# A hybrid recurrent and attention layer pair in split float32r: the low part of each weight from an adding DMA instead of a VectorE subtraction

## The chip, the cores and the metric

The kernel runs on one core of a Trainium2 chip. The core has five engines that work side by side, each through its own queue in order: TensorE (PE in the profile, with its weight loads as PEld), VectorE (DVE), ScalarE (ACT), GpSimd (POOL) and SyncE (SP). SP, ACT and POOL can issue DMAs; all of these run on the core's 16 DMA engines. The metric is the time of one execution on the device in microseconds (us).

## The reference

The reference is a trunk of two pre-norm residual layers for 512 tokens of 2048 features, in float32. Cut to what matters here:

```python
h = rms_norm(x, rec_norm)                      # layer 0
proj = h @ rec_w_in                            # 2048 x 12288
rg_x, rg_g, hg_q, hg_f, hg_i, hg_g = split(proj)
y_rg = rg_lru(conv4(rg_x), w_a, b_a, w_x, b_x, lam) * silu(rg_g)       # 8 heads of 256
y_hg = rms_norm(hgrn2(hg_q, sigmoid(-hg_f), hg_i, log_sigmoid(hg_f))) * silu(hg_g)   # 16 heads of 128
x = x + concat(y_rg, y_hg) @ rec_w_out         # 4096 x 2048
h = rms_norm(x, att_norm)                      # layer 1
q, k, v, g = split(h @ att_w_in)               # 2048 x 8192
y = sub_norm(diff_attention(rope(norm(q)), rope(norm(k)), v, lam)) * silu(g)
out = x + y @ att_w_out                        # 2048 x 2048
```

Nearly all of the arithmetic is in the four large products with `rec_w_in`, `rec_w_out`, `att_w_in` and `att_w_out`.

## The kernel before

**Products in two parts.** The kernel multiplies in float32r. To lose less to its rounding, it splits each operand into a high part (rounded to float32r) and a low part (the rest, again in float32r), and each product is made of three: high by high, high by low, low by high. `mm3` issues the three matmuls (L104, L105, L106).

**Weights.** The weights lie in DRAM in chunks of 128 x 1024 float32 (512 KB), in order of use. `raw` (L80 to L85) loads a chunk from SP into one of three `wraw` buffers. A chunk has two halves of 128 x 512, and each half is one **step**. `split` (L87 to L93) makes the two parts of a half: ScalarE rounds it into `whi` (L91), VectorE subtracts `whi` from it into `wlo` (L92). `whi` and `wlo` have five buffers each, used in rotation: a new split takes the buffer of the fifth split before it, and can be written only when TensorE has read that one for the last time.

**Projections.** A step is 12 matmuls of 128 x 512, four groups of three. In `proj_feat` (256 output features) the weight is the stationary operand, and L106 is the first to read `wlo`. In `proj_tok` (512 output features) the weight is the moving operand, and L105, the second matmul of the step, is the first to read `wlo`. There are 832 steps: 256 for HGRN2 and 128 for RG-LRU (`w_rec`), 128 for the first output projection (`w_rout`), 256 for attention (`w_att`) and 64 for the last output projection (`w_aout`). The 8 gate chunks of RG-LRU (`w_gate`, in `rg_head`) have 16 halves more, so 848 halves are split in all.

**The two output projections.** There the left operand is split just in time as well: `jit_split` runs the head outputs `y` (named `ya`, `yb`, `y` in the profile) through the same `split`, once for each step. So in these 192 steps two splits are made for a step, weight first and then `y`, out of the same five buffers, and five splits are only two and a half steps. A weight takes the buffer of the `y` of three steps before; a `y` takes the buffer of the weight of two steps before. In all other steps a weight takes the buffer of the weight of five steps before.

**Order.** Between the steps, `tick` lets generators issue the heads' own work (decays, scores, softmax, norms) in small pieces, so that it lies among the projections' matmuls on TensorE. The framework's scheduler orders instructions on each engine; both instructions of `split` are issued with high priority. At the start, TensorE multiplies dummies, the input is loaded transposed in eight DMAs from SP (`yb<-in_xT`) and split into `h` on ScalarE and VectorE (L744, L745), the first three weight chunks are loaded between them, and `prepare` loads the input a second time in eight DMAs from POOL (`yb<-in_x`, L165) for the row norms, in three buffers in rotation, squaring each on ScalarE (L166). These eight are all that POOL's queue holds besides four small memsets.

Of the kernel before, what the change touches and what calls it, by code (L numbers as in the profile page):

```python
# [10 lines left out]
F32R = mybir.dt.float32r  # L11
# [3 lines left out]
ALU = mybir.AluOpType  # L15
# [4 lines left out]
P = 128  # L20
# [14 lines left out]
SUB_EPS = 1e-5  # L35
# steps of the heads' own work between two half chunks of a projection
TICK_HG, TICK_RG, TICK_OUT, TICK_ATT = 2, 2, 3, (1.5, 1.5, 2, 1.2)
LEVELS = (32, 16, 8, 4, 2)

# columns of the packed per-feature parameters  # L40
C_G0, C_CW, C_CB, C_BA, C_BX, C_LAM, C_HGN, C_G1, C_SUB = 0, 16, 80, 96, 112, 128, 144, 145, 161
N_COL = 163
# columns of the packed parameters that are repeated for every partition
R_QN, R_KN = 0, 128
N_ROW = 256
N_LP = 4 * 128
# columns of the packed constants
K_ID, K_COS, K_SIN, K_NEG = 0, 128, 192, 256
# [3 lines left out]
class Kernel:  # L52
# [8 lines left out]

# [1 line left out]
    def tick(self, n):  # L63
# [14 lines left out]

# [1 line left out]
    def raw(self, src):  # L80
        if self.raws and self.use_raws:
            return self.raws.pop(0)
        t = self.wp.tile([P, CH], F32, name="wraw", bufs=3)
        self.nc.sync.dma_start(t, src)
        return t  # L85

# [21 lines left out]
    def rsqrt(self, pool, ss, n, scale, eps):  # L108
        """(ss * scale + eps) ** -0.5 on a few columns"""
        nc = self.nc  # L110
        V = nc.vector
        m = pool.tile([P, n], F32, name="rs_m")
        y = pool.tile([P, n], F32, name="rs_y")
        t = pool.tile([P, n], F32, name="rs_t")
        V.tensor_scalar(t, ss, scale, eps, op0=ALU.mult, op1=ALU.add)
        V.tensor_scalar(m, t, -0.5, None, op0=ALU.mult)
        # first guess from the bits, then Newton until float32 has converged
        V.tensor_scalar(y.bitcast(I32), t.bitcast(I32), -0.5, 1597463007.0, op0=ALU.mult, op1=ALU.add)
        for _ in range(3):
            V.tensor_tensor(t, y, y, op=ALU.mult)  # L120
            V.tensor_tensor(t, t, m, op=ALU.mult)
            V.scalar_tensor_tensor(y, t, 1.5, y, op0=ALU.add, op1=ALU.mult)
        return y

# [1 line left out]
    def proj_feat(self, h, src, chunk0, ticks):  # L126
        """256 output features as two [feature, token] banks"""
        ps = [self.pj.tile([P, S], F32, name="pj") for _ in range(2)]
        for c in range(4):
            raw = self.raw(src[chunk0 + c])  # L130
            for s in range(2):
                w = self.split(raw[:, s * HALF:(s + 1) * HALF])
                for kk in range(2):
                    kt = 4 * c + 2 * s + kk
                    for o in range(2):
                        sl = slice(kk * 256 + o * P, kk * 256 + (o + 1) * P)
                        self.mm3(ps[o], (w[0][:, sl], w[1][:, sl]), h[kt], kt == 0, kt == KD - 1)
                self.tick(ticks)
        return ps

    def proj_tok(self, lhs, order, src, chunk0, ticks):
        """512 output features as four [token, feature] banks; lhs(kt) gives the split activations"""
        ps = [self.pj.tile([P, S], F32, name="pj") for _ in range(NT)]
        n = len(order)
        for c in range(n // 2):
            raw = self.raw(src[chunk0 + c])
            for s in range(2):
                i = 2 * c + s
                w = self.split(raw[:, s * HALF:(s + 1) * HALF])
                a = lhs(order[i])  # L150
                for tt in range(NT):
                    sl = slice(tt * P, (tt + 1) * P)
                    self.mm3(ps[tt], (a[0][:, sl], a[1][:, sl]), w, i == 0, i == n - 1)
                self.tick(ticks)
        return ps

    def prepare(self):
        """1 / rms of each token, as columns and as a row repeated for every partition; small constants"""
        nc = self.nc
# [34 lines left out]

# [1 line left out]
    def hgrn_head(self, hd, qs, f, sg, v, vc):  # L196
        nc, wk, sm, pm = self.nc, self.wk, self.sm, self.pm
        V = nc.vector
        # the lower bound is a softmax over one layer less its first row: it is zero
        # for these shapes, so log_f = log_sigmoid(f) and k = sigmoid(-f)  # L200
        lf = wk.tile([P, S], F32, name="lf")
# [8 lines left out]
        yield  # L210
        # the scale of q goes with k
        V.scalar_tensor_tensor(lnk, lf, HG_LOG_SCALE, f, op0=ALU.add, op1=ALU.subtract)
# [3 lines left out]
        yield  # L216
        # s = t, and s = t - 1 for odd t: products summed over the features by ones
        x = wk.tile([P, 768], F32, name="so")
# [63 lines left out]
        for li, h in enumerate(LEVELS[1:], 1):  # L282
# [3 lines left out]
            yield  # L286
        # pairs of 64-token chunks: k decayed to the end of its even chunk, q from the start of
        # its odd one; then both for the 128-token chunks, which meet through a running state
        kp = wk.tile([P, S], F32, name="kp")
# [110 lines left out]

# [1 line left out]
    def rg_lambda(self):  # L402
        """-8 * softplus(-lambda), with log1p as 2 atanh(e / (2 + e))"""
        nc, sm = self.nc, self.sm
        V = nc.vector
        lam = self.col[:, C_LAM:C_LAM + 16]
        e = sm.tile([P, 16], F32, name="lm_e", bufs=1)
        t = sm.tile([P, 16], F32, name="lm_t", bufs=1)
        t2 = sm.tile([P, 16], F32, name="lm_t2", bufs=1)
        a = sm.tile([P, 16], F32, name="lm_a", bufs=1)  # L410
        c = self.cp.tile([P, 16], F32, name="crg")
        nc.scalar.activation(e, lam, AF.Abs)
        nc.scalar.activation(e, e, AF.Exp, scale=-1.0)
        V.tensor_scalar(t, e, 2.0, None, op0=ALU.add)
        V.reciprocal(t, t)
        V.tensor_tensor(t, t, e, op=ALU.mult)
        V.tensor_tensor(t2, t, t, op=ALU.mult)
        V.memset(a, 1.0 / 17)
        for i in (15, 13, 11, 9, 7, 5, 3, 1):
            V.tensor_tensor(a, a, t2, op=ALU.mult)  # L420
            V.tensor_scalar(a, a, 1.0 / i, None, op0=ALU.add)
        V.tensor_tensor(a, a, t, op=ALU.mult)
        V.tensor_scalar(c, lam, -1.0, 0.0, op0=ALU.mult, op1=ALU.max)
        V.scalar_tensor_tensor(c, a, 2.0, c, op0=ALU.mult, op1=ALU.add)
        V.tensor_scalar(c, c, -8.0, None, op0=ALU.mult)
        self.crg = c

    def rg_head(self, hd, xr, sg):
# [5 lines left out]
        for ct in range(2):  # L434
# [13 lines left out]
            xs.append((hi, lo))  # L448
            w.append(self.split(wg[:, ct * HALF:(ct + 1) * HALF]))
            yield  # L450
# [20 lines left out]
        for jt in range(2):  # L471
            m, i = ri[jt]
            nc.scalar.activation(m, a[jt], AF.Square)
            # -expm1(2 y) = -tanh(y) (1 + exp(y)^2)
            V.scalar_tensor_tensor(m, m, 1.0, th[jt], op0=ALU.add, op1=ALU.mult)
# [35 lines left out]

# [1 line left out]
    def att_prep(self, q, k, ssq, ssk):  # L513
# [25 lines left out]
    def att_pair(self, pr, q, k, v, box):  # L539
# [7 lines left out]
        def heads_in(hh):  # L547
            """split transposes of a head's q and k"""
            for x, dst, nm in ((q, qT, "q"), (k, kT, "k")):
# [100 lines left out]
    def attention(self, h):  # L650
        nc = self.nc
        ch = 0
        for pr in range(ATT_HEADS // 2):
            got, sss = [], []
            for job, nm in enumerate("qkvg"):
                ps = self.proj_tok(lambda kt: h[kt], list(range(KD)), self.w_att, ch, TICK_ATT[job])
                ch += 8
                # q, k and the gate take turns in two buffers
                if job == 1:
# [32 lines left out]

# [1 line left out]
    def jit_split(self, kt):  # L694
        return self.split(self.y[kt])

    def run(self):
# [20 lines left out]
        with ExitStack() as st:  # L718
            self.ybp = pool(st, "ybp")
            self.rio = pool(st, "rio")  # L720
            xs = []
            # products that nothing reads warm the array up while the first loads are under way
            wm = self.rio.tile([P, S], BF16, name="xr0")
# [41 lines left out]

            # x1 = x + y @ w_out, its split transpose times the gain, and its mean squares
            ss1 = self.cp.tile([P, NT, 4], F32, name="ss1")
# [82 lines left out]
def feat_chunks(w, c0):  # L850
    """[2048, 256] at column c0 -> 4 chunks of four k tiles"""
    return w[:, c0:c0 + 256].reshape(4, 4, P, 256).transpose(0, 2, 1, 3).reshape(4, P, CH)


def tok_chunks(w, c0, order=None):
    """[k, 512] at column c0 -> chunks of two k tiles, in the order of use"""
    k = w.shape[0] // P
# [6 lines left out]
def layout(x, rec_norm, rec_w_in, rg_conv_w, rg_conv_b, rg_w_gate_a, rg_b_gate_a, rg_w_gate_x, rg_b_gate_x,  # L864
# [11 lines left out]
    for hd in range(RG_HEADS):  # L876
        rec.append(feat_chunks(w, hd * 256))
        rec.append(feat_chunks(w, 2048 + hd * 256))
    gate = np.stack([rg_w_gate_a[0], rg_w_gate_x[0]], 1)                     # head, gate, i, j
    gate = gate.reshape(RG_HEADS, 2, 2, P, 256).transpose(0, 3, 2, 1, 4).reshape(RG_HEADS, P, CH)  # L880
# [40 lines left out]
```

## Time and profile before

| | us |
|---|---|
| runs of the kernel | 2596.36, 2596.66, 2597.73; median 2596.66 |
| span of the profiled execution, first to last instruction | 2594.6 |
| VectorE busy | 1417.0 (55%) |
| ScalarE busy | 1258.6 (49%) |
| GpSimd busy | 4.6 |

The page of the profile gives the span of its execution; the time around it is the 2.1 us by which the median of the runs is longer. Clock of TensorE in the mean: 0.998 of full.

How to read it: busy time says how long an engine worked, not whether anyone waited for it. The lists of waits say who waited for whom. The groups of instructions are given by line of the kernel, output and inputs, with the mean duration of one. A DMA's time to landing runs from its issue to the completion of its data. The stage windows give busy time, the granted clock and the mean busy share of the DMA engines in each stretch of the span. Matmuls are pipelined: one follows another in 0.22 to 0.23 us, though the row of one shows 0.39.

### The profile page before, as it was taken

What the parts mean: (1) busy time and instruction counts of PE and PEld (TensorE: products, weight loads), DVE (VectorE), ACT (ScalarE), POOL (GpSimd) and SP (SyncE); (2) the same over time, 40 slices, a digit from 0 to 9 for tenths busy, and PEclk for the clock granted to TensorE, in tenths of its full rate; (3) what the DMA queues carried; (4) which work ended last, traced back from release to release, by engine and by line L of the source; (5) the groups of instructions that cost most, each with busy time, mean ns of one, the idle gap of its engine ahead of it and who ended that gap; (6) DMA issues with size and microseconds to landing.
All of it is one profiled execution on the core that took longest, in us unless ns stands there. A gap on an engine that the chain in (4) does not pass through costs nothing.

```text
span 2594.6 us, 33221 instructions
## 1 busy us (share of the span) xinstructions
PE 2579.6 (99%) x12416; PEld 2126.2 (82%) x12416; DVE 1417.0 (55%) x3073; ACT 1258.6 (49%) x2458; POOL 4.6 (0%) x12
## 2 busy tenths in 40 slices
PE   9999999999999999999999999999999999999999
PEld 7888888888888888888888888888888888888887
DVE  5466557646646665545654555344544534544654
ACT  8445545535444455556544444334434434534543
POOL 0000000000000000000000000000000000000000
PEclk9999999999999999999999999999999999999999
DMA  6222222222222222222232333222222222222243
GB/s 244 96 74 82 81 82 74 81 90 74 76 95 74 74 98 102 97 93 98 90 128 95 127 130 120 98 98 75 81 97 77 79 91 82 76 95 93 86 146 114
DMA packets 73457, 250.48 MB, mean 97 GB/s; under 512 B 8144, under 2 KB 8656, under 8 KB 73296
## 3 DMA queue, kind: packets, MB, share of 16 engines
q1 hardware_dynamic: 71712, 243.58, 26.8%
q0 software_dynamic: 1152, 4.19, 0.4%
q8 instruction: 97, 1.59, 0.2%
q10 hardware_dynamic: 432, 0.59, 0.1%
q14 instruction: 64, 0.52, 0.1%
HBM read 239.95 MB, written 8.39 MB: 96 GB/s over the span
## 4 chain that ended last, share of the span: by engine, by line
PE 94%; DVE 2%; ACT 2%; DMA 1%; issue 1%; SPq 0%; ACTq 0%
PE pj L104 28%; PE pj L106 28%; PE pj L105 28%; PE pm L258 2%; PE pm L570 1%; PE pm L104 1%; PE pm L106 1%; PE pm L105 1%; PE pm L343 1%; PE pm L554 1%; DMA yb<-in_x 0%; PE pm L332 0%; PE pm L345 0%; ACT a L675 0%; PE pm L359 0%
## 5 line engine op out<-in xcount | busy, mean ns | idle before, releaser
L92 DVE TENSOR_TENSOR wlo<-wraw,whi 128x512 fp32r<-128x512 f32 x848 | 582.3, 688 | 671.4 <-ACT whi L91 641.2
L91 ACT CAST whi<-wraw 128x512 fp32r<-128x512 f32 x848 | 523.0, 618 | 765.0 <-PE pj L106 463.7
L106 PE MATMUL pj<-whi,wlo 128*128 128x512 f32 x768 | 299.6, 390 | 0.0
L105 PE MATMUL pj<-wlo,whi 128*128 128x512 f32 x768 | 299.4, 390 | 0.0
L104 PE MATMUL pj<-whi 128*128 128x512 f32 x768 | 299.3, 390 | 0.0
L106 PEld LDWEIGHTS pj<-whi,wlo 128*128 128x128 f32 x768 | 144.2, 188 | 30.5 <-DVE wlo L92 0.6
L104 PEld LDWEIGHTS pj<-whi 128*128 128x128 f32 x768 | 144.2, 188 | 30.4 <-issue 0.5
L105 PEld LDWEIGHTS pj<-wlo,whi 128*128 128x128 f32 x768 | 144.2, 188 | 29.1
L240 ACT ACTIVATE e<-e 128x512 f32<-128x512 f32 x80 | 50.5, 632 | 131.7 <-DVE e L239 97.6
L92 DVE TENSOR_TENSOR wlo<-ya,whi 128x512 fp32r<-128x512 f32 x64 | 44.3, 693 | 89.9 <-ACT whi L91 89.9
L92 DVE TENSOR_TENSOR wlo<-y,whi 128x512 fp32r<-128x512 f32 x64 | 44.2, 691 | 82.3 <-ACT whi L91 82.3
L91 ACT CAST whi<-ya 128x512 fp32r<-128x512 f32 x64 | 39.7, 621 | 100.9 <-PE pj L105 100.9
L91 ACT CAST whi<-y 128x512 fp32r<-128x512 f32 x64 | 39.9, 623 | 94.1 <-PE pj L105 90.2
L92 DVE TENSOR_TENSOR wlo<-yb,whi 128x512 fp32r<-128x512 f32 x64 | 44.1, 690 | 72.2 <-ACT whi L91 72.0
L91 ACT CAST whi<-yb 128x512 fp32r<-128x512 f32 x64 | 39.8, 621 | 76.5 <-PE pj L105 76.5
L258 PEld LDWEIGHTS pm<-e 128*128 128x128 f32 x512 | 66.6, 191 | 5.0 <-DVE e L241 0.3
L258 PE MATMUL pm<-e 128*128 128x128 f32 x512 | 67.5, 275 | 0.0
L241 DVE TENSOR_TENSOR e<-e,hin 128x256 f32<-128x256 f32 x80 | 33.6, 420 | 58.8 <-ACT e L240 58.8
L575 ACT ACTIVATE p<-pm,mx 128x128 f32<-128x128 f32 (+3 forms) x64 | 33.7, 526 | 40.6 <-DVE mx L573 38.6
L572 DVE TENSOR_REDUCE mx<-pm 128x1 f32<-128x128 f32 (+3 forms) x64 | 30.4, 485 | 32.6 <-PE pm L571 32.3
L675 ACT ACTIVATE a<-pj,rstd 128x128 f32<-128x128 f32 x128 | 47.3, 421 | 0.3
L104 PE MATMUL pj<-h0h,whi 128*128 128x512 f32 x80 | 33.8, 423 | 5.2 <-DVE hin L384 2.9
(474 smaller groups left out, 6483.0 us busy)
## 6 DMA issues: line engine op xcount, KB each, us to landing
wraw<-in_w_rec SPq DMA_DIRECT2D x192, 512.0 KB, 3.2
wraw<-in_w_att SPq DMA_DIRECT2D x128, 512.0 KB, 3.2
wraw<-in_w_rout SPq DMA_DIRECT2D x64, 512.0 KB, 3.2
wraw<-in_w_aout SPq DMA_DIRECT2D x32, 512.0 KB, 3.2
yb<-in_xT SPq DMA_DIRECT2D x8, 512.0 KB, 8.5
yb<-in_x POOLq DMA_DIRECT2D x8, 512.0 KB, 5.5
wraw<-in_w_gate SPq DMA_DIRECT2D x8, 512.0 KB, 3.2
xo<-in_x SPq DMA_DIRECT2D x16, 256.0 KB, 4.0
```

The lines of the kernel that those rows point to most:

```text
L91: self.nc.scalar.copy(hi, src)
L92: self.nc.vector.tensor_tensor(lo, src, hi.bitcast(F32), op=ALU.subtract)
L104: mm(out, a[0], b[0], start=start, stop=False)
L105: mm(out, a[0], b[1], start=False, stop=False)
L106: mm(out, a[1], b[0], start=False, stop=stop)
L240: nc.scalar.activation(e, e, AF.Exp)
L241: V.tensor_tensor(e1, e1, vw(qs, h)[:, :, 1, :], op=ALU.mult)
L258: nc.tensor.matmul(ps[:, sl], e[:, sl], e[:, sl], start=True, stop=True)
L343: nc.tensor.matmul(po[:, sl], st[:, sl], v[:, t, vc:vc + P], start=True, stop=t == 0)
L572: V.tensor_reduce(mx[:, i:i + 1], ps[:, :n], axis=AX.X, op=ALU.max)
L575: nc.scalar.activation(e[:, :n], ps[:, :n], AF.Exp, scale=ATT_SCALE, bias=mx[:, i:i + 1], accum_out=z[:, i:i + 1])
L675: nc.scalar.activation(x[:, t, g * P:(g + 1) * P], ps[t][:, g * P:(g + 1) * P], AF.Square, scale=r1, accum_out=ss[:, t * 4 + g:t * 4 + g + 1])
```

## The change

The weights are split in another way, in a function of its own. ScalarE first writes the negative of the raw half into `wlo`, rounded to float32r, and rounds the half into `whi` as before. Then POOL issues a DMA that reads the same half once more from DRAM and adds it to what stands in `wlo`: weight minus rounded weight, the same low part. VectorE no longer takes part for the 848 weight halves. The `y` splits of the two output projections keep the old `split`. `raw` now also hands on where in DRAM the chunk comes from.

```diff
     def raw(self, src):
...
         self.nc.sync.dma_start(t, src)
-        return t
+        return t, src
+
+    def wsplit(self, raw, s):
+
+        t, src = raw
+        sl = slice(s * HALF, (s + 1) * HALF)
+        hi = self.wp.tile([P, HALF], F32R, name="whi", bufs=5)
+        lo = self.wp.tile([P, HALF], F32R, name="wlo", bufs=5)
+        with self.tc.high_priority():
+            self.nc.scalar.mul(lo, t[:, sl], -1.0)
+            self.nc.scalar.copy(hi, t[:, sl])
+            self.nc.gpsimd.dma_start(lo, src[:, sl], accum_op=ALU.add)
+        return hi, lo
...
     def proj_feat(self, h, src, chunk0, ticks):
...
-                w = self.split(raw[:, s * HALF:(s + 1) * HALF])
+                w = self.wsplit(raw, s)
...
     def proj_tok(self, lhs, order, src, chunk0, ticks):
...
-                w = self.split(raw[:, s * HALF:(s + 1) * HALF])
+                w = self.wsplit(raw, s)
...
     def rg_head(self, hd, xr, sg):
...
-            w.append(self.split(wg[:, ct * HALF:(ct + 1) * HALF]))
+            w.append(self.wsplit(wg, ct))
```

The diff also drops comments; lines behind the new function stand 12 lower. The old `split` is L99 to L105 in the new file, with its rounding at L103 and its subtraction at L104; the negative is L94, the rounding of a weight L95, the adding DMA L96.

Three places in the order of instructions show what moves. The first is ScalarE's queue in the first output projection, four steps of it, before: a weight is rounded, then the `y` of the same step, in turn (numbers behind a name tell its buffers' users apart).

```order
L91 CAST whi_12282<-wraw_12280 128x512
L91 CAST whi_12286<-ya0_7917 128x512
L91 CAST whi_12302<-wraw_12280 128x512
L91 CAST whi_12306<-ya1_7921 128x512
L91 CAST whi_12324<-wraw_12322 128x512
L91 CAST whi_12328<-ya2_8293 128x512
L91 CAST whi_12344<-wraw_12322 128x512
L91 CAST whi_12348<-ya3_8297 128x512
```

The same place on ScalarE now:

```order
L95 CAST whi_12762<-wraw_12760 128x512
L94 ACTIVATE wlo_12763<-wraw_12760 128x512
L103 CAST whi_12767<-ya0_8197 128x512
L95 CAST whi_12783<-wraw_12760 128x512
L94 ACTIVATE wlo_12784<-wraw_12760 128x512
L103 CAST whi_12788<-ya1_8201 128x512
L95 CAST whi_12806<-wraw_12804 128x512
L94 ACTIVATE wlo_12807<-wraw_12804 128x512
L103 CAST whi_12811<-ya2_8591 128x512
```

Each step has a third instruction on ScalarE, and the adding DMA follows on the second of them.

The second place is POOL's queue at the start of the program, before: only the second loads of the input.

```order
L165 DMA yb5_353<-in_x 128x1024
L165 DMA yb6_356<-in_x 128x1024
L165 DMA yb7_375<-in_x 128x1024
L165 DMA yb5_378<-in_x 128x1024
L165 DMA yb6_399<-in_x 128x1024
```

POOL's queue at the start now, from the fifth adding DMA on:

```order
L96 DMA wlo_271<-in_w_rec 128x512
L96 DMA wlo_288<-in_w_rec 128x512
L177 DMA yb5_362<-in_x 128x1024
L177 DMA yb6_365<-in_x 128x1024
L96 DMA wlo_307<-in_w_rec 128x512
L96 DMA wlo_324<-in_w_rec 128x512
L96 DMA wlo_345<-in_w_rec 128x512
L96 DMA wlo_369<-in_w_rec 128x512
L96 DMA wlo_394<-in_w_rec 128x512
L177 DMA yb7_385<-in_x 128x1024
L177 DMA yb5_388<-in_x 128x1024
L96 DMA wlo_417<-in_w_rec 128x512
```

The rows begin with the fifth and sixth of the adding DMAs; the seventh stands behind two loads of the input that wait for their buffers, the twelfth behind four. After the last load of the input the queue holds adding DMAs alone, 848 in all.

The third place is ScalarE at the start, now: where the two halves of the first chunk were rounded one after the other, both negatives come first.

```order
L756 ACTIVATE h0h_79<-yb0_132,col_134 128x512
L756 ACTIVATE h1h_81<-yb0_132,col_134 128x512
L94 ACTIVATE wlo_203<-wraw_136 128x512
L94 ACTIVATE wlo_220<-wraw_136 128x512
L95 CAST whi_202<-wraw_136 128x512
L95 CAST whi_219<-wraw_136 128x512
L756 ACTIVATE h2h_83<-yb1_138,col_134 128x512
```

So the first `whi` moved behind two new instructions. TensorE's own sequence of matmuls is the same but for small shifts of the heads' pieces.

## The prediction, made before the change was run

> **What bounds the kernel now.** First the head of the page: who is busy, and the chain that ended last.
>
> ```profile
> span 2594.6 us, 33221 instructions
> PE 2579.6 (99%) x12416; PEld 2126.2 (82%) x12416; DVE 1417.0 (55%) x3073; ACT 1258.6 (49%) x2458; POOL 4.6 (0%) x12
> ...
> PE 94%; DVE 2%; ACT 2%; DMA 1%; issue 1%; SPq 0%; ACTq 0%
> ```
>
> TensorE works 2579.6 of 2594.6 us, and 94% of the chain is its. Whatever is taken from VectorE can give back at most the 15.0 us in which TensorE stands. The list of TensorE's waits tells who causes these:
>
> ```profile
> PE pj L104 <- DVE hin L384: 3.2, 2, 2.9
> PE pj L104 <- ACT whi L91: 2.2, 1, 2.2
> PE pm L359 <- DVE kp L354: 1.5, 9, 0.3
> ```
>
> No wait of matmuls for `wlo` stands there. The groups by line say the same of the subtraction that goes:
>
> ```profile
> L92 DVE TENSOR_TENSOR wlo<-wraw,whi 128x512 fp32r<-128x512 f32 x848 | 582.3, 688 | 671.4 <-ACT whi L91 641.2
> L91 ACT CAST whi<-wraw 128x512 fp32r<-128x512 f32 x848 | 523.0, 618 | 765.0 <-PE pj L106 463.7
> L106 PEld LDWEIGHTS pj<-whi,wlo 128*128 128x128 f32 x768 | 144.2, 188 | 30.5 <-DVE wlo L92 0.6
> ```
>
> 848 subtractions take 582.3 us of VectorE, yet 768 weight loads waited 0.6 us in all for `wlo`. VectorE makes the low part early. The question of this change is therefore not what VectorE saves, but **how early**: whether the slower way through a DMA still fits into the head start that five buffers give.
>
> **The head start in the output projections.** I read it from the timeline of the first of them, for ScalarE and TensorE. ScalarE's rows:
>
> ```profile
> 1301.80 0.62 ACT L91 CAST whi<-ya 128x512 fp32r<-128x512 f32 x1 [1.58 <-PE pj L105]
> 1302.33 0.62 ACT L91 CAST whi<-wraw 128x512 fp32r<-128x512 f32 x1
> ```
>
> TensorE's rows:
>
> ```profile
> 1301.60 0.39 PE L106 MATMUL pj<-whi,wlo 128*128 128x512 f32 x1
> 1301.83 0.39 PE L104 MATMUL pj<-whi 128*128 128x512 f32 x1
> ...
> 1304.55 0.39 PE L104 MATMUL pj<-whi 128*128 128x512 f32 x1
> ...
> 1307.27 0.39 PE L104 MATMUL pj<-whi 128*128 128x512 f32 x1
> 1307.49 0.39 PE L105 MATMUL pj<-wlo,whi 128*128 128x512 f32 x1
> ```
>
> Steps begin at 1301.83, 1304.55 and 1307.27, so a step is 2.72 us. As the step before 1301.83 ends, two buffers come free; ScalarE rounds the `y` of the next but one step at 1301.80 and at 1302.33 the weight of the step at 1307.27 (this weight takes the buffer of the `y` of three steps before). Its `wlo` is first read by L105 at 1307.49.
>
> Now: the negative follows the rounding by ScalarE's own pace, 0.53 us (1301.80 to 1302.33), and lasts about as long as the rounding, 0.62. It ends at 1302.33 + 0.53 + 0.62 = 1303.48. I allow 0.1 us for the handover to POOL (an estimate; the timeline has such gaps between engines). The DMA may then take, from issue to landing, 1307.49 - 1303.48 - 0.1 = **3.9 us** without anybody waiting. If it takes L, two steps last at least L plus what lies around it: 2T + 0.22 = 1.66 + 0.1 + L, so T = (1.54 + L)/2.
>
> In the other 640 steps a weight has its buffer four steps ahead, 4 x 2.72 = 10.9 us; less the same 1.8, the DMA may take some 9 us. Only the splits that share the rotation with gate weights have less.
>
> **What an adding DMA takes.** None is in the trace. The nearest rows, from the list of DMA issues and the loads from POOL:
>
> ```profile
> wraw<-in_w_rout SPq DMA_DIRECT2D x64, 512.0 KB, 3.2
> yb<-in_xT SPq DMA_DIRECT2D x8, 512.0 KB, 8.5
> yb<-in_x POOLq DMA_DIRECT2D x8, 512.0 KB, 5.5
> xo<-in_x SPq DMA_DIRECT2D x16, 256.0 KB, 4.0
> ```
>
> ```profile
> L165 POOL DMA_DIRECT2D yb<-in_x x8: 527/527/664, 21.3 to 39.3; - x8
> ...
> DMA to landing us min/median/max: 4.3/5.5/6.9
> ```
>
> Each moves 256 KB, but must read them and the 256 KB that stand in `wlo`: the traffic of reading is that of the 512 KB loads from POOL, which landed in 4.3 to 6.9 us beside busy DMA engines. The bound below is the 3.2 us of a chunk from SP, the bound above the 8.5 us of the crowded start; ends of 3.2 and 8.5, then. The stage windows say how crowded it is:
>
> ```profile
> core 0: us, PE busy (x) PEld busy (x) DVE busy (x) ACT busy (x) POOL busy (x), PEclk, DMA share, GB/s
> 0.00:30.00 30.00, 26.56 (x102) 19.57 (x103) 22.80 (x60) 25.12 (x38) 2.45 (x8) 0.94 0.86 320
> ...
> 920.00:1250.00 330.00, 330.00 (x1451) 271.99 (x1450) 188.33 (x294) 184.87 (x274) 0.00 (x0) 1.00 0.28 97
> 1250.00:1615.00 365.00, 365.00 (x1640) 301.99 (x1639) 194.70 (x305) 179.56 (x326) 0.00 (x0) 1.00 0.33 116
> ```
>
> and the queue's own row how long the engines are held:
>
> ```profile
> q1 hardware_dynamic: 71712, 243.58, 26.8%
> ```
>
> 243.58 MB take 26.8% of 2594.6 us, 695 us, on all 16 engines; 256 KB (0.262 MB) so take 0.75 us, and with two reads, as I estimate, 1.5 us. In an output projection the share of 0.33 grows by 1.5 in a step of 3.2 us, to some 0.75: between quiet and the start. So I take the middle between the shortest and the median load from POOL, **L = 4.9 us**.
>
> On the second read the Trainium skill has a rule, in "Collectives: The Full Stack", Part 3: a reducing step is half as fast as a copy because it needs two source reads, not because of the add. No trace here shows an add; by that rule an adding DMA holds the engines 1.5 us, without it 0.75.
>
> **The sum.**
>
> *Output projections.* T = (1.54 + 4.9)/2 = 3.22 us, 0.50 more than 2.72, in 128 + 64 = 192 steps: **+96 us**. With L = 3.2 it is 0, with 8.5 T = 5.02 and +442. What is queued behind the wait is all of TensorE: L105 of a step holds every later matmul, and so also the reading that would free the next buffers; that is why the delay repeats in each step rather than being paid once.
>
> *Other 640 steps.* 4.9 is below 9: **0**, hidden behind four steps of products. If L passes 9, T is about (1.8 + L)/4.
>
> *Start.* The first matmuls and the first low part:
>
> ```profile
> 8.00 0.57 PE L104 MATMUL pj<-h0h,whi 128*128 128x512 f32 x1 [2.24 <-ACT whi L91]
> ...
> 9.65 1.05 PE L106 MATMUL pj<-h0h,wlo 128*128 128x512 f32 x2
> ```
>
> Two negatives of 0.53 now stand ahead of the first `whi`, so L104 begins 1.1 us later. The first `wlo` lands not after one 0.69 us subtraction but after a DMA between eight loads that take 8.5 us each; with 4.3 to 8.5 after a negative that ends at about 8.0, it lands at 12.3 to 16.5, where 9.65 was wanted: 3 to 7 us. Further on POOL holds adding DMAs behind the second loads of the input, which wait for buffers and for squares on ScalarE and were issued from 21.3 to 39.3 us; the seventh low part, which stands behind two of them, cannot be issued before about 24. I take **+10**, ends 3 and 30.
>
> *ScalarE.* 848 negatives at the price of its nearest row,
>
> ```profile
> L240 ACT ACTIVATE e<-e 128x512 f32<-128x512 f32 x80 | 50.5, 632 | 131.7 <-DVE e L239 97.6
> ```
>
> are 536 us; the order has 19 more table loads, 1.28 us each by
>
> ```profile
> L205 ACT ACT_TABLE_LOAD x12 | 15.4, 1283 | 1.4 <-PEq L911 1.2
> ```
>
> that is 24. ScalarE comes to 1258.6 + 536 + 24 = 1819 us, 70% of the span. In its fullest long stage (920 to 1250) 184.87 and some 136 x 0.63 = 86 make 82%. TensorE's products hide it: **0**. If heads' pieces come late, TensorE's waits for them, now a few us, could grow; bound +30.
>
> *VectorE.* 582 us fewer, gain bounded by the waits shown above: 3.2 + 1.5 us. I take 0.
>
> *Weight loads from SP.* A chunk's buffer comes free after ScalarE's second reading instead of VectorE's; both come right on the buffer's turn: 0.
>
> Sum: 2594.6 + 96 + 10 = 2700.6 in the span, with the 2.1 us around it **2703 us**, 4.1% more than the median of 2596.66.
>
> **The rivals.**
>
> *Covered (not slower).* If an adding DMA lands within 3.9 us, no step waits, and of the change only the start is left. The decision lies at L = 3.9. For it speaks the 3.2 us of a 512 KB chunk from SP, in the same stage; against it that all eight loads from POOL took 4.3 or more, and that the raw chunks share the engines. Start at its lower end of 3, less up to 4.7 us of waits for VectorE: 2595 to 2600 us; with the start as priced, 2607. The Trainium skill, "DMA: Bandwidth & Descriptors", section "Anatomy of one DMA", gives 2.0 us and the bytes by 436 GB/s for a DMA from GpSimd, which is 2.6 us for 256 KB and 3.2 for 512 KB, and would put this case ahead; the loads from POOL here, 4.3 to 6.9 us for 512 KB, are longer than it says.
>
> *The DMA engines become the bound.* Raw chunks take 0.75 us of the engines in each step, so 1.97 of 2.72 are left; above that each of the 848 adding DMAs costs time in every stage, however early it is issued. This takes an add 2.6 times as long as a plain 256 KB move. If it is four times, 3.0 us, the engines need 695 + 848 x 3.0 = 3239 us, so about 3250. For it: nothing in the trace shows an adding DMA at any rate, and if the engine reads, adds and writes one row after another, it may be slow. Against it: with two reads at the copy rate it comes to 1.5, and the share to 26.8% + 49%.
>
> *ScalarE falls behind.* With 70 to 82% busy and in order, a negative that waits for a buffer holds the heads' work behind it, and TensorE waits for heads' pieces in the stages of HGRN2 and RG-LRU as well. 30 us of that over covered steps give about 2637. For it: three instructions for two in each output step; against it: the waits for ScalarE are now 2.2 + 0.9 us in 2594.
>
> *The change does not do what it says*: the order shows all 848 subtractions of weights gone from VectorE and 848 adding DMAs on POOL; this rival is closed.
>
> **How the numbers follow.** The forecast, waits in the output projections alone, has 0.58. Within it L from 4.2 to 6.4 gives +29 to +240 and with the start 2630 to 2850. Covered has 0.12, half of it within 0.2% of the median (some 5 us, about what a measurement of this kernel can tell from no change), a quarter faster; the DMA engines as bound, or L beyond 9, 0.22; ScalarE 0.08. The range from 2603 leaves out about 0.08 below, and to 3050 some 0.12 above, half of the slow DMA case. Faster by over 0.2% 0.03, within 0.06, slower 0.91.
>
> **What would show it.** In the profile after: TensorE waiting for the DMA `wlo` at L105, nearly all of it in the two output projections, with steps of about 3.2 us; adding DMAs landing in 4 to 6 us; the adding queue holding the engines for some 50% of the span at 1.5 us for each DMA; VectorE 582 us lighter and ScalarE near 1820. Waits for `wlo` spread over all stages, with the DMA share near 1, would show the engines as bound; waits for ScalarE the third rival; no waits behind the first 50 us the covered case. The forecast would be most wrong if an add is far slower in the DMA engine than two reads.

## The result, and the profile after

The changed kernel takes **2763.82 us** (median of four runs, 2758.42 to 2765.12) against 2596.51 us of the kernel before in the same session: 1.064 times as long, 95% interval 1.0625 to 1.0655. The forecast was 2703 us with a range of 2603 to 3050; the direction and the place were right, the size was too small by 61 us.

The head of the page after, its chain, its DMA queues, and the groups that belong to a weight's split (columns as before):

```profile
span 2763.3 us, 35169 instructions
PE 2629.2 (95%) x12416; PEld 2126.8 (77%) x12416; DVE 893.1 (32%) x2225; ACT 1718.6 (62%) x3325; POOL 740.3 (27%) x860
...
q0 software_dynamic: 123264, 226.55, 47.8%
q1 hardware_dynamic: 71712, 243.58, 30.6%
...
PE 66%; DMA 13%; issue 13%; POOL 4%; ACT 2%; DVE 2%; POOLq 0%; SPq 0%; DVEq 0%; ACTq 0%
...
L94 ACT ACTIVATE wlo<-wraw 128x512 fp32r<-128x512 f32 x848 | 530.0, 628 | 370.1 <-PE pj L117 357.2
L95 ACT CAST whi<-wraw 128x512 fp32r<-128x512 f32 x848 | 516.1, 610 | 192.8 <-PE pj L117 152.7
...
wlo<-in_w_rec POOLq DMA_DIRECT2D x384, 256.0 KB, 5.3
...
wlo<-in_w_rout POOLq DMA_DIRECT2D x128, 256.0 KB, 5.1
...
wlo<-in_w_aout POOLq DMA_DIRECT2D x64, 256.0 KB, 5.0
```

VectorE is 524 us lighter and ScalarE 460 us heavier. TensorE's share of the chain fell from 94% to 66%; DMAs, GpSimd and the time in which no wait is told ("issue") took its place. Over the span no engine is full, and the DMA engines are at 78%: TensorE now stands for 134.1 us, after 15.0 before. Its list of waits says for what (total, times, longest):

```profile
PE pj L117 <- DMA wlo<-in_w_rout: 65.1, 53, 2.6
PE pj L117 <- DMA wlo<-in_w_aout: 34.0, 23, 4.1
PE pj L118 <- DMA wlo<-in_w_rec: 10.2, 9, 6.1
PE pj L116 <- DVE hin L396: 5.9, 1, 5.9
PE pj L116 <- ACT a L694: 4.7, 5, 1.7
```

L116 to L118 are the three matmuls that were L104 to L106; L117 is the first to read `wlo` in an output projection. Every step has twelve of the projections' matmuls, so the steps can be counted on TensorE and the span cut where the stages begin: after 16 steps, then HGRN2, RG-LRU, first output projection, attention, last output projection. The stage windows of before:

```profile
core 0: us, PE busy (x) PEld busy (x) DVE busy (x) ACT busy (x) POOL busy (x), PEclk, DMA share, GB/s
0.00:56.80 56.80, 50.43 (x209) 39.14 (x209) 32.81 (x88) 48.12 (x69) 4.56 (x12) 0.96 0.74 277
56.80:842.30 785.50, 784.04 (x4095) 649.22 (x4096) 470.14 (x1064) 387.01 (x707) 0.00 (x0) 1.00 0.23 81
842.30:1249.60 407.30, 406.87 (x1884) 335.41 (x1883) 242.59 (x424) 222.16 (x347) 0.00 (x0) 1.00 0.27 93
1249.60:1610.20 360.60, 360.60 (x1617) 298.19 (x1616) 190.91 (x296) 175.16 (x314) 0.00 (x0) 1.00 0.33 112
1610.20:2400.10 789.90, 788.00 (x3737) 647.78 (x3736) 373.19 (x996) 338.59 (x852) 0.00 (x0) 1.00 0.25 89
2400.10:2594.60 194.50, 189.71 (x885) 156.46 (x883) 107.34 (x210) 87.57 (x174) 0.00 (x0) 1.00 0.33 115
```

The same stages after:

```profile
0.00:70.60 70.60, 52.98 (x209) 39.16 (x209) 20.18 (x67) 52.21 (x85) 23.14 (x33) 0.91 1.00 291
70.60:855.10 784.50, 782.76 (x4095) 648.59 (x4096) 321.89 (x825) 531.50 (x961) 207.06 (x239) 1.00 0.77 162
855.10:1266.60 411.50, 408.79 (x1883) 334.80 (x1882) 155.96 (x284) 294.01 (x487) 121.48 (x140) 1.00 0.84 182
1266.60:1721.10 454.50, 388.99 (x1624) 299.39 (x1623) 114.19 (x166) 246.14 (x448) 114.48 (x132) 0.98 0.76 164
1721.10:2519.20 798.10, 790.23 (x3730) 646.26 (x3728) 209.47 (x739) 472.24 (x1110) 220.38 (x255) 1.00 0.80 172
2519.20:2763.30 244.10, 205.41 (x884) 158.61 (x883) 71.44 (x148) 122.45 (x238) 53.73 (x62) 0.97 0.72 159
```

The second number is the length of a stage. The 168.7 us more in the span are:

| stage | us more |
|---|---|
| start and first 16 steps | +13.8 |
| rest of HGRN2 | -1.0 |
| RG-LRU | +4.2 |
| first output projection, 128 steps | +93.9 |
| attention | +8.2 |
| last output projection, 64 steps | +49.6 |

143.5 of them lie in the two output projections, 0.73 and 0.78 us for each step. HGRN2 runs the same adding DMAs, with the DMA engines 77% busy, and loses nothing. Only in the first 70.6 us are the DMA engines full (1.00).

### The profile page after: what moved, and what is told of

Same layout as the page of the kernel before. It is cut to its first block, busy times and chain, and to the rows that moved or that the text cites. A ratio compares the mean times of both kernels' runs of the same rounds, so it can differ in the third digit from the quotient of the medians.

```text
span 2763.3 us, 35169 instructions
## 1 busy us (share of the span) xinstructions
PE 2629.2 (95%) x12416; PEld 2126.8 (77%) x12416; DVE 893.1 (32%) x2225; ACT 1718.6 (62%) x3325; POOL 740.3 (27%) x860
## 3 DMA queue, kind: packets, MB, share of 16 engines
q0 software_dynamic: 123264, 226.55, 47.8%
## 4 chain that ended last, share of the span: by engine, by line
PE 66%; DMA 13%; issue 13%; POOL 4%; ACT 2%; DVE 2%; POOLq 0%; SPq 0%; DVEq 0%; ACTq 0%
PE pj L117 20%; PE pj L118 19%; PE pj L116 19%; DMA wlo<-in_w_rout 7%; POOL wlo L96 3%; DMA wlo<-in_w_aout 3%; PE pm L270 2%; DMA wlo<-in_w_rec 1%; DMA wlo<-in_w_att 1%; PE pm L582 1%; PE pm L355 1%; ACT wlo L94 0%; PE pm L344 0%; PE pm L357 0%; PE pm L371 0%
## 5 line engine op out<-in xcount | busy, mean ns | idle before, releaser
L94 ACT ACTIVATE wlo<-wraw 128x512 fp32r<-128x512 f32 x848 | 530.0, 628 | 370.1 <-PE pj L117 357.2
L95 ACT CAST whi<-wraw 128x512 fp32r<-128x512 f32 x848 | 516.1, 610 | 192.8 <-PE pj L117 152.7
L96 POOL DMA_DIRECT2D wlo<-in_w_rec x384 | 333.2, 877 | 874.6 <-ACT wlo L94 807.1
L117 PE MATMUL pj<-wlo,whi 128*128 128x512 f32 x768 | 316.8, 413 | 99.7 <-DMA wlo<-in_w_rout 65.1
L96 POOL DMA_DIRECT2D wlo<-in_w_att x256 | 222.1, 882 | 570.0 <-ACT wlo L94 543.6
L118 PE MATMUL pj<-whi,wlo 128*128 128x512 f32 x768 | 306.4, 399 | 0.0
L116 PE MATMUL pj<-whi 128*128 128x512 f32 x768 | 303.0, 397 | 0.1
L117 PEld LDWEIGHTS pj<-wlo,whi 128*128 128x128 f32 x768 | 147.4, 192 | 169.5 <-DMA wlo<-in_w_rout 93.5
L96 POOL DMA_DIRECT2D wlo<-in_w_rout x128 | 111.3, 875 | 334.9 <-ACT wlo L94 316.9
L116 PEld LDWEIGHTS pj<-whi 128*128 128x128 f32 x768 | 147.2, 192 | 32.7 <-ACT whi L103 0.4
L118 PEld LDWEIGHTS pj<-whi,wlo 128*128 128x128 f32 x768 | 147.7, 192 | 27.9
L103 ACT CAST whi<-y 128x512 fp32r<-128x512 f32 x64 | 39.7, 621 | 111.3 <-PE pj L117 107.8
L103 ACT CAST whi<-ya 128x512 fp32r<-128x512 f32 x64 | 39.6, 619 | 110.1 <-PE pj L117 110.1
L96 POOL DMA_DIRECT2D wlo<-in_w_aout x64 | 55.5, 872 | 194.3 <-ACT wlo L94 148.8
L104 DVE TENSOR_TENSOR wlo<-ya,whi 128x512 fp32r<-128x512 f32 x64 | 44.3, 693 | 169.1 <-ACT whi L103 169.1
L103 ACT CAST whi<-yb 128x512 fp32r<-128x512 f32 x64 | 39.7, 620 | 95.3 <-PE pj L117 95.3
L104 DVE TENSOR_TENSOR wlo<-yb,whi 128x512 fp32r<-128x512 f32 x64 | 44.3, 692 | 160.4 <-ACT whi L103 160.2
L104 DVE TENSOR_TENSOR wlo<-y,whi 128x512 fp32r<-128x512 f32 x64 | 44.3, 692 | 155.2 <-ACT whi L103 155.2
L285 DVE TENSOR_TENSOR st<-pm,cst 128x512 f32<-128x512 f32 x16 | 11.0, 690 | 207.6 <-PE pm L284 207.6
```

What stands on the lines that cost most here:

```text
L94: self.nc.scalar.mul(lo, t[:, sl], -1.0)
L95: self.nc.scalar.copy(hi, t[:, sl])
L96: self.nc.gpsimd.dma_start(lo, src[:, sl], accum_op=ALU.add)
L103: self.nc.scalar.copy(hi, src)
L104: self.nc.vector.tensor_tensor(lo, src, hi.bitcast(F32), op=ALU.subtract)
L116: mm(out, a[0], b[0], start=start, stop=False)
```

## The experiments

All ratios are to the kernel before in the same session; diffs are against the changed kernel unless another is named.

**Where the loss sits: the adding DMA in all but the output projections, and in them alone.** The first:

```diff
+    def wold(self, raw, s):
+        return self.split(raw[0][:, s * HALF:(s + 1) * HALF])
...
-    def proj_tok(self, lhs, order, src, chunk0, ticks):
+    def proj_tok(self, lhs, order, src, chunk0, ticks, out=False):
...
-                w = self.wsplit(raw, s)
+                w = self.wold(raw, s) if out else self.wsplit(raw, s)
...
-                ps = self.proj_tok(lhs, order, self.w_rout, 16 * n, 1)
+                ps = self.proj_tok(lhs, order, self.w_rout, 16 * n, 1, True)
...
-                ps = self.proj_tok(lhs, list(range(KD)), self.w_aout, 8 * n, TICK_OUT)
+                ps = self.proj_tok(lhs, list(range(KD)), self.w_aout, 8 * n, TICK_OUT, True)
```

> The two output projections (192 steps) keep VectorE's subtraction; all other weights use the adding DMA. Head-start theory: the loss sits where weight and y share five buffers, 93.8 us in the first and 49.6 us in the second output projection of the profiles, so 2764 - 143 = about 2620 us, within 10. Rival, the load theory (each adding DMA costs by its load on the DMA engines and on ScalarE, wherever it is): 656 of 848 adding DMAs remain and so 656/848 of the loss of 167 us, 2597 + 129 = 2726 us.

Measured: 2621.23 us, 1.0097 (1.0081 to 1.0112). The reverse, `wsplit` if `out`, else `wold`, and `wold` in `proj_feat` and for the gate weights too:

> The reverse: the adding DMA only in the two output projections, VectorE's subtraction everywhere else, the start included. Head-start theory: 2597 + 143 = about 2740 us, with 3.5 us a step in these stages. Load theory: 192 of 848 adding DMAs, 2597 + 38 = 2635 us.

Measured: 2736.61 us, 1.054 (1.0524 to 1.0555). Both land within 4 us of the head-start theory and over 100 us from the load theory. The two output projections last 361.6 and 194.4 us in the first and 449.2 and 241.4 in the second. 192 adding DMAs make 84% of the loss, the other 656 the rest.

**Same instructions and DMAs, more head start.** The `y` splits get buffers of their own (tiles of `h` that are not needed at that time), and the weights have the five to themselves:

```diff
     def jit_split(self, kt):
-        return self.split(self.y[kt])
+        src = self.y[kt]
+        j = self.jn = (self.jn + 1) % 3
+        hi = self.hp.tile([P, HALF], F32R, name=f"h{12 + j}h")
+        lo = self.hp.tile([P, HALF], F32R, name=f"h{12 + j}l")
+        with self.tc.high_priority():
+            self.nc.scalar.copy(hi, src)
+            self.nc.vector.tensor_tensor(lo, src, hi.bitcast(F32), op=ALU.subtract)
+        return hi, lo
...
-            h1 = [tuple(self.hp.tile([P, S], F32R, name=f"h{kt}{hl}") for hl in "hl") for kt in range(KD)]
+            h1 = []
+            self.jn = 0
...
                     g = self.col[:, C_G1 + kt:C_G1 + kt + 1]
+                    h1.append(tuple(self.hp.tile([P, S], F32R, name=f"h{kt}{hl}") for hl in "hl"))
```

> Every weight by the adding DMA, as in the change, but the y splits of the output projections take three buffers of their own (tiles of h that are dead in those stages), so a weight there has its buffer four steps ahead instead of two. Same instructions, same DMAs. Head-start theory: the waits for wlo in the output projections go, 2764 - 143 = 2620 to 2630 us. Load theory and the theory that the third instruction on ScalarE slows these steps: 2764 us, nothing changes.

Measured: 2624.99 us, 1.0112 (1.0097 to 1.0127). The stage windows of the two output projections:

```profile
1266.30:1628.90 362.60, 361.71 (x1624) 299.09 (x1623) 114.16 (x166) 243.06 (x446) 112.51 (x131) 1.00 0.88 207
...
2426.80:2622.10 195.30, 189.87 (x884) 156.65 (x882) 70.12 (x146) 119.90 (x234) 51.85 (x60) 1.00 0.80 198
```

362.6 and 195.3 us, within 2 us of before, although the DMA engines are busier there (0.88) than in the change (0.76) and ScalarE does the same work. So neither the load nor ScalarE's third instruction makes the loss; the short head start does.

**How many buffers it takes.** On top of that kernel, four and then three buffers for the weights:

```diff
     def wsplit(self, raw, s):
...
-        hi = self.wp.tile([P, HALF], F32R, name="whi", bufs=5)
-        lo = self.wp.tile([P, HALF], F32R, name="wlo", bufs=5)
+        hi = self.wp.tile([P, HALF], F32R, name="whi", bufs=4)
+        lo = self.wp.tile([P, HALF], F32R, name="wlo", bufs=4)
...
```

The same two numbers change in `split`, which shares these buffers.

> The kernel with buffers of their own for y, and four instead of five for the weights: every weight has its buffer three steps ahead, not four. Head-start theory: 3 x 2.72 = 8.2 us less the 1.9 us to the issue and plus the 0.2 us to the second product leave 6.4 us for the add, which lands in 5.3 us in the mean and 7 us at most times: few waits, 2625 to 2660 us.

> The same with three buffers for the weights: two steps ahead in all 832 steps, as the output projections have in the change. Head-start theory: the output projections lose again what they lose in the change, about 143 us, and now the other 640 steps lose as well, some 0.3 to 0.5 us each as far as the heads' work among them does not cover it (their steps last 3.1 to 3.3 us in the mean): 2625 + 143 + 190 to 320 = about 2950 to 3090 us. Load theory, in which the buffers do not matter: 2625 us for both.

Measured: 2702.24 us with four, 1.0403 (1.0386 to 1.042), and 2939.46 with three, 1.1317 (1.1301 to 1.1334). The load theory is out again, but both expectations missed: 2702 lies above the 2660 of the first, 2939 below the 2950 of the second. With four, RG-LRU took 452.6 us and attention 823.7, against 411.5 and 797.9 with five. I had counted neither the gate weights, which hold two of the weights' buffers over several steps, nor the late landings; how much each of these makes was not separated. With three, the stages are:

```profile
888.20:1413.90 525.70, 447.45 (x1883) 346.78 (x1882) 154.61 (x284) 299.00 (x492) 122.68 (x142) 0.95 0.67 143
1413.90:1806.90 393.00, 372.28 (x1624) 297.29 (x1624) 114.24 (x166) 246.25 (x448) 113.16 (x132) 1.00 0.83 192
1806.90:2720.00 913.10, 830.51 (x3729) 659.24 (x3727) 210.31 (x741) 474.72 (x1111) 220.99 (x256) 0.97 0.71 149
2720.00:2939.30 219.30, 197.60 (x884) 158.92 (x882) 70.17 (x146) 122.26 (x238) 53.58 (x62) 0.98 0.75 181
```

Against five buffers RG-LRU and attention lose 114 and 115 us and HGRN2 28, but the output projections 30 and 24, not the 143 I had expected of two steps' head start. ScalarE's rows there tell why, first of this kernel, then of the change:

```profile
1502.00 0.63 ACT L94 ACTIVATE wlo<-wraw 128x512 fp32r<-128x512 f32 x1 [2.35 <-PE pj L117]
1502.54 0.60 ACT L712 CAST h12h<-ya 128x512 fp32r<-128x512 f32 x1
1503.05 0.62 ACT L95 CAST whi<-wraw 128x512 fp32r<-128x512 f32 x1
```

```profile
1399.40 0.62 ACT L103 CAST whi<-yb 128x512 fp32r<-128x512 f32 x1 [2.82 <-PE pj L117]
1399.92 0.61 ACT L95 CAST whi<-wraw 128x512 fp32r<-128x512 f32 x1
1400.44 0.62 ACT L94 ACTIVATE wlo<-wraw 128x512 fp32r<-128x512 f32 x1
```

Here the negative comes first as the buffer comes free, in the change third, 1.0 us later. By pairing each DMA with its step in the first output projection, its issue comes 1.33 us after the buffer is free, against 2.23 in the change, and its landing 4.7 us later, against 5.2. The prediction's rule, T = (issue - 0.22 + landing)/2, gives 2.92 us for a step; 393.0/128, less the 0.10 that transposes take between steps, is 2.97. That it comes so near is chance, since the rule counts a wait too few, as the part on the prediction shows: with three waits counted it gives 2.85, and the waits for `wlo` that the profile names there, 19.1 us in 128 steps, make 2.87. The other 0.1 us is named as no wait.

**The order on ScalarE in the change itself.** VectorE rounds the high part, so that only the `y` stands ahead of the negative:

```diff
-            self.nc.scalar.copy(hi, t[:, sl])
+            self.nc.vector.tensor_copy(hi, t[:, sl])
```

> The change with the high part of a weight rounded on VectorE instead of ScalarE, so that in the output projections ScalarE has only the rounding of y ahead of the negative and the adding DMA is issued some 0.5 us earlier after the buffer comes free (1.4 instead of 1.9 us). Head-start theory, T = (issue - 0.22 + landing)/2: 0.26 us less in each of 192 steps, 2764 - 50 = about 2714 us, and a few us more back elsewhere from ScalarE's lighter load. Rival, that the earlier issue is lost again because copies on VectorE hold up GpSimd or the DMA: landing in w_rout above 5.1 us at the median and 2740 to 2764 us.

Measured: 2740.32 us, 1.0552 (1.0534 to 1.057). The issue came 0.5 us earlier, as meant (1.77 after 2.23), and the output projections took 439 and 228 us, 31 less together rather than 50. The rival's two figures came true, 5.3 us at the median of `w_rout` and just over 2740 us, but its reason does not explain the output projections: there GpSimd still starts the issue 0.29 us after the negative, landing is only 0.1 us later in the mean (5.29 after 5.21), and a rounding on VectorE overlaps the issue in only 4 of 192 steps. The 50 us came from a rule that is too steep (see the part on the prediction). Attention instead grew from 798 to 815 us, with 18.2 us of waits for `wlo` where the change has 1.9. There the rival may hold: the 25 of its 256 issues that overlap a rounding on VectorE land in 7.2 us in the mean, the others in 5.6, and 12 of the 18 us are waits for these 25. No run separates that from other reasons.

**What an adding DMA consists of: a plain copy in its place.** `wlo` is overwritten, nothing is added:

```diff
-            self.nc.gpsimd.dma_start(lo, src[:, sl], accum_op=ALU.add)
+            self.nc.gpsimd.dma_start(lo, src[:, sl])
```

> The change with a plain DMA in place of the adding one: wlo is overwritten with the weight (rounded to float32r on the way), the addition is left out, all else as it is. In the profile of the change a 2 KB packet of the adding queue holds an engine 178 ns at the median, a plain 2 KB packet 84 ns. Theory that the second read makes it: packets of about 84 ns, landing some 0.7 us earlier (median of w_rout 4.4 instead of 5.1 us), steps of the output projections shorter by half of that, 192 x 0.35 = 67 us, about 2697 us. Rival, that rounding to float32r or the way through GpSimd makes the packet slow: 178 ns, 5.1 us and 2764 us stay.

Measured: 2667.03 us, 1.0279 (1.0263 to 1.0294). The queue and the issues:

```profile
q0 software_dynamic: 123264, 226.55, 30.7%
...
wlo<-in_w_rout POOLq DMA_DIRECT2D x128, 256.0 KB, 3.7
```

GpSimd's rows of the copy, then of the adding DMA in the change (ns, shortest, median, longest):

```profile
L96 POOL DMA_DIRECT2D wlo<-in_w_rout x128: 527/527/537, 1249.4 to 1650.8; - x128
```

```profile
L96 POOL DMA_DIRECT2D wlo<-in_w_rout x128: 866/866/1223, 1258.0 to 1710.9; - x128
```

Adding costs twice: GpSimd takes 0.34 us longer to issue, and a packet of 2 KB holds an engine 178 ns at the median, not 99. All in all it lands 1.4 us later, twice the 0.7 expected, and the kernel without it is 97 us faster, 85 of them in the output projections. A plain copy from SP of the same packet size takes 84 ns; what of the 15 ns more is the rounding was not separated.

**Why every second step waits longer.** In the first output projection of the change, steps take 3.07 and 4.03 us in turn, and the DMAs of first and second halves land in 4.6 and 5.9 us (means over the DMAs of each half). A chunk loaded in two halves into six buffers:

```diff
-        t = self.wp.tile([P, CH], F32, name="wraw", bufs=3)
-        self.nc.sync.dma_start(t, src)
+        t = [self.wp.tile([P, HALF], F32, name="wraw", bufs=6) for _ in range(2)]
+        for s in range(2):
+            self.nc.sync.dma_start(t[s], src[:, s * HALF:(s + 1) * HALF])
...
-            self.nc.scalar.mul(lo, t[:, sl], -1.0)
-            self.nc.scalar.copy(hi, t[:, sl])
+            self.nc.scalar.mul(lo, t[s], -1.0)
+            self.nc.scalar.copy(hi, t[s])
```

> The change with each raw chunk loaded as two halves of 256 KB into six buffers, so each half is released and reloaded by itself. In the profile of the change the adding DMAs of the second half of a chunk land 1.3 us later than those of the first (5.87 against 4.55 us in the first output projection). Theory that this is the collision with the 512 KB load that the second half's release triggers: the two become alike, near 5.2 us, even and odd steps become alike, and the time stays within 30 us of 2764, lower if at all, as the longest waits and the halved clock behind them get rarer. Rival, that the order on ScalarE or POOL makes the second half late: the 1.3 us stay.

Measured: 2736.70 us, 1.0545 (1.052 to 1.057); landings of 5.1 and 5.0 us, steps of 3.48 and 3.39. So the later landing is a collision: ScalarE's second negative of a chunk releases the chunk's buffer and the adding DMA in the same moment, and 512 KB from SP share the engines with it. From another side, the add taken from `wraw` in SBUF, which holds the raw buffer until it has landed:

```diff
-            self.nc.gpsimd.dma_start(lo, src[:, sl], accum_op=ALU.add)
+            self.nc.gpsimd.dma_start(lo, t[:, sl], accum_op=ALU.add)
```

> The change with the adding DMA reading the raw half from wraw in SBUF instead of from DRAM. Now a raw buffer is released only when the add has landed, so the 512 KB load can no longer start together with the add of the second half. Collision theory: adds of both halves land alike, near the 4.55 us of the first half in the change, steps of (1.94 - 0.22 + 4.55)/2 = 3.1 us, 192 x 0.41 less than now, about 2685 us. Rival, that what counts is the amount of DMA work alone: landing 5.2 us in the mean and about 2764 us, or 2737 as with half loads.

Measured: 2713.53 us, 1.0457 (1.044 to 1.0473). The landings became alike (4.3 and 4.1 us in the first output projection) and shorter than expected, but the gain was 50 us, not 79. Two things change at once here, where the DMA reads and when the buffer is released, so this run alone does not show the collision. Some DMAs still landed late (7 to 8 us in the worst steps), and the longest waits had a further price that is shown below.

**The start, and ScalarE's part of the rest.** On top of the kernel with buffers for `y`, VectorE's subtraction in the first 16 steps:

```diff
     def proj_feat(self, h, src, chunk0, ticks):
...
-                w = self.wsplit(raw, s)
+                w = self.wold(raw, s) if src is self.w_rec and chunk0 < 8 else self.wsplit(raw, s)
```

> The kernel with buffers of their own for y, and VectorE's subtraction for the first 16 steps as well. The start theory (the first adding DMAs land late among the input loads, and stand in POOL's queue behind the second loads of the input): the 12 to 14 us lost up to step 16 come back, 2625 - 13 = 2612 us. Rival, that the start only waits for the DMA engines and the loss moves behind it: 2620 to 2625 us.

Measured: 2613.22 us, 1.0066 (1.0049 to 1.0083): 12 us come back, 10.7 of them up to step 16. And on top of the same kernel the negative on VectorE:

```diff
-            self.nc.scalar.mul(lo, t[:, sl], -1.0)
+            self.nc.vector.tensor_scalar(lo, t[:, sl], -1.0, None, op0=ALU.mult)
```

> The kernel with buffers of their own for y, with the negative made on VectorE instead of ScalarE (so ScalarE has the load of the kernel before, and VectorE its old load nearly). Theory that the 8 us lost in attention are ScalarE's: TensorE waits for a at the end of a projection fall from 5.5 us to below 1, and the time to about 2617 us. Rival, that they come from the DMA or from late low parts: 2625 us. If VectorE's instruction holds up the issue on GpSimd, adding DMAs take longer to land and it is slower than 2625.

Measured: 2618.00 us, 1.0087 (1.0072 to 1.0102). The sum came as expected but not from attention: the waits for `a` went, but attention took 798.9 us after 797.9, while its waits for `wlo` rose from 2.4 to 5.5 us. The 4 us by which the span of this profile is shorter lie mostly in the start and RG-LRU. So where the 8 us in attention come from is not settled; the add itself is not the reason, as the kernel with the plain copy takes 797.9 us there too. In RG-LRU that kernel takes 407.4 us and so loses nothing. No version tried is faster than the kernel before; the best, 2613 us, still is 0.66% slower.

## Why the prediction was right, and where its size was off

**The bound.** That VectorE's subtraction was hidden and its removal brings nothing was right: 524 us of VectorE went, and no stage got shorter by more than the 1.0 us of HGRN2.

**Output projections, forecast +96, measured +143.** This is the term that was mis-sized. That the short head start makes the loss is shown by three kernels; the sum for it had four errors, and that it came as near as it did is in part luck.

- *Landing.* L was taken as 4.9 us, and is 5.2 in the mean of `w_rout` (5.1 at the median): I had not seen that the chunk's load from SP starts together with every second adding DMA.
- *Issue.* The time from the free buffer to the issue was taken as 1.66 + 0.1 us. The handover from ScalarE to GpSimd alone is 0.29 us, and the issue comes 1.94 us after the buffer at the median, 2.23 in the mean. So the decision between loss and none lies not at L = 3.9 but at 3.4 to 3.7.
- *The rule.* T = (1.54 + L)/2 has two waits between the free buffer and the landing, and there are three. The buffer comes free as the step two before begins; `wlo` is read at the second matmul of its own step, and each of these three steps waits there. So three steps together last as long as issue, landing and the 2.50 us of a step behind that matmul: T = (1.76 + L + 2.50)/3. With L = 4.9 that is 3.05 us, +64 and not +96. The trace bears it out: in the 27 steps of the last output projection that waited, issue and landing take 1.86 us more in the mean than two undisturbed steps and a matmul, and three waits together make 1.78, the first two alone 0.47.
- *What a wait brings behind it* was put at nothing. The waits that the profile names are 99 of the 143 us; the other 44 are TensorE's own busy time, 388.99 after 360.60 and 205.41 after 189.71 us. 15 of them are matmuls at half clock (last section). The rest is not separated.

With L = 5.2 the rule of three steps gives 3.21 us and +95 for the median issue of 1.94 us, 3.31 us and +113 for the mean of 2.23, against the 99 us of waits; the prediction's rule gives 3.6 us and +170 for the mean. Mostly only every second step waits: in the first output projection the first half of a chunk lands 0.9 us before it is read (median), the second half just as it is read.

**Engine time, forecast 1.5 us for each add.** 47.8% of 2763.3 us less 10 us for the loads of `yb`, by 848, is 1.55 us; the plain copy, 30.7% of 2670.0, takes 0.95, not the 0.75 that was doubled. So the match is in part luck as well: an add holds the engines 1.6 times as long as the copy, its packets 1.8 times. The rule that a reducing step costs two reads and the add itself nothing (the Trainium skill, "Collectives: The Full Stack", Part 3) fits roughly: by it the factor would be two. That rule is on bandwidth; this kernel pays for latency, of which it says nothing.

**Start, forecast +10, measured +13.8.** The first wait came where it was expected:

```profile
9.49 0.40 PE L117 MATMUL pj<-h0l,whi 128*128 128x512 f32 x1
15.97 1.22 PE L118 MATMUL pj<-h0h,wlo 128*128 128x512 f32 x2 [6.08 <-DMA wlo<-in_w_rec]
```

The first `wlo` landed at 15.97 us, within the 12.3 to 16.5 of the forecast.

**Other steps, forecast 0, measured +11.4**, of which RG-LRU and attention have 12.4 and HGRN2 -1.0: small, and in part unexplained.

**ScalarE**, forecast 1819 us, 1718.6 measured: instructions that follow each other start 0.53 us apart and overlap at their ends, so 848 of them add less busy time than their durations. That it stays hidden was right. The 82% for 920 to 1250 us counted some 136 halves there; the trace before has 119.

**The rivals.** Covered: the median landing of the adding DMAs is 5.3 us, above the 3.9 from which it decides, though the shortest is 3.6. Even the plain copy, 3.7 us at the median of `w_rout`, left 59 us of loss in the output projections: its second halves took 4.2 us. The DMA engines as the bound: at 78% they are not, but for the start, and the kernel with buffers for `y` runs them at 0.88 in a stage without loss. ScalarE falling behind: up to some us, as above.

## What to carry to other kernels

Before work is moved off an engine, look at who waits for its result: a subtraction that nobody waits for cannot be sped up, it can only be made late. Count the head start of a buffer rotation in steps, and count every user of the rotation: a second user halves it, and a slower producer then stalls where a faster one never showed. When the wait repeats in each step, count each wait that lies between the buffer's release and the reading. The adding DMA in place of VectorE's instruction held DMA engines that had room (1.55 us of all 16) and took 5.3 us to land, and it landed later still when the event that issued it also released a load.

## What the runs showed of the hardware that I had not expected

TensorE's clock halved for 3.4 us behind some single waits of 1.9 us and more, so such a wait cost more than itself. In the change, around one of the waits for `wlo`:

```profile
1401.67 0.50 PE L117 MATMUL pj<-wlo,whi 128*128 128x512 f32 x1 [1.86 <-DMA wlo<-in_w_rout]
1402.01 0.40 PE L118 MATMUL pj<-whi,wlo 128*128 128x512 f32 x1
1402.24 0.39 PE L116 MATMUL pj<-whi 128*128 128x512 f32 x1
1402.47 0.51 PE L117 MATMUL pj<-wlo,whi 128*128 128x512 f32 x1
1402.78 0.63 PE L118 MATMUL pj<-whi,wlo 128*128 128x512 f32 x1
1403.21 0.63 PE L116 MATMUL pj<-whi 128*128 128x512 f32 x1
```

Matmuls follow each other in 0.23 us, then in 0.43. The granted clock of the stage is 0.98 in the first and 0.97 in the last output projection after, 1.00 in both before. The slow matmuls (0.35 to 0.5 us apart) take 15 us more in the two stages than at the full pace, a tenth of their loss. The trace's record of the clock changes on a grid of 3.41 us, and nine stretches of this grid in the two stages are at half clock. In the stretch just before each of them TensorE stood 55 to 94% of the time, for one wait of 1.9 to 4.1 us; no stretch of the two stages in which it stood 52% or less was followed by one. The Trainium skill, "TensorE: Matmul & The Clock Gate", Part 1, puts halving behind idle windows of about 3.4 us. This trace does not agree: one wait of 1.86 us, as above, was enough where it filled over half of such a stretch.
